# A NaN-skipping row maximum: packed 16-bit keys in a tile of their own, and loads of seven rows

## The chip, the cores and the metric

The kernel runs on one core of a Trainium2 chip. The metric is the device time of one execution, in microseconds (us). The kernel before takes 1284.18 us, the median of three runs (1283.97 to 1284.49).

Of the core's engines three compute here: ScalarE (ACT in the profile), GpSimd (POOL) and VectorE (DVE). SyncE (SP) issues all transfers, loads and stores, in one queue and in program order.

## The reference

The input is a float32 array of 32 x 2048 rows of 2048 numbers, in which about one number in ten is a NaN. The output is the maximum of each row, with NaNs left out:

```python
x = np.random.randn(32, 2048, 2048).astype(np.float32)
x[np.random.rand(32, 2048, 2048) < 0.1] = np.nan

def reference(x, axis):            # axis = -1
    return np.nanmax(x, axis=axis).astype(np.float32)
```

That is 537 MB read for 0.26 MB written. A row that holds nothing but NaNs gives a NaN.

## The kernel before

The 65536 rows are spread over 128 partitions, so that each partition has 512 rows of 8 KB. From here on "a row" means one row in every partition, which is 128 x 8 KB = 1.05 MB of the input.

**How a NaN is made harmless.** [...] the kernel first turns each NaN into the lowest number. It does this on the upper 16 bits of each float (the "key"); the lower 16 bits stay where they are. As a 16-bit integer the key of a NaN (0x7FC0) lies above that of every finite positive number (at most `TOP` = 0x7F7F).

1. ScalarE (L94) reads the key as int16, computes `TOP + 0.25 - key`, multiplies it by a slope `alpha` where it is negative, which is the case for NaNs alone, and writes the result as uint16. `alpha` is chosen so that every NaN gives the one value `TOP + 129`.
2. GpSimd (L102) reads that as uint16, computes `TOP - value` and writes an int16. This gives ordinary keys back unchanged and turns a NaN's key into -129, which is 0xFF7F, the upper half of a very large negative float.
3. VectorE (L110) takes the float32 maximum along each row into `acc`.

Both key steps work in place: they read and write every second 16-bit number of the loaded tile, `[:, 1::2]`, 4 bytes apart. At the end of a group of rows VectorE finds the rows that held only NaNs ("none", L118) and sets bits so that they become NaN ("fin", L127).

**How the work is tiled.** `GROUPS` is a list of groups; a group is a list of tiles, a tile a list of loads, and a load a list of pieces, in rows. A tile is one buffer of `WIDE` = 8 rows (64 KB per partition) of the pool `io`, which has three. Nearly all of the work is tiles of one load of 8 rows, worked on in pieces of 3, 3 and 2 rows: 12 groups of 5 such tiles (40 rows each) and one group of one. The last 24 rows are three groups of one tile each, with loads of 4, 2 or 1 rows and pieces of 2 or 1.

**What sets the order.** Each engine works through its instructions in order and waits for what they need. A piece goes from ScalarE to GpSimd to VectorE. A load into a buffer waits until VectorE has reduced all pieces that the buffer held before, three tiles back. Stores are put off: after each load, if more than one group's result is waiting to be stored, SyncE issues the oldest of these stores (L91) before it issues the next load (L86). A store waits for its group's "fin", and all later loads wait behind it in SyncE's queue. The last stores are at L132.

The functions with their line numbers:

Of the kernel before, what the change touches and what calls it, by code (L numbers as in the profile page):

```python
# [1 line left out]

# [4 lines left out]

FULL = [[3, 3, 2]]
GROUPS = [[FULL] * 5] * 12 + [
    [FULL],
    [[[2, 2], [2], [2]]],
    [[[2], [2], [1], [1], [1], [1]]],
    [[[1], [1], [1], [1], [1], [1], [1], [1]]],
]
WIDE = 8

TOP = 0x7F7F
NAN = 0x7FC0
LOW = -129

EDGE = TOP + 0.25

NONE = -255.0 * 2.0**120


@with_exitstack
def kernel(
    ctx: ExitStack,
    tc: tile.TileContext,
    x: bass.AP,
    axis: bass.AP,
    out: bass.AP,
):

    nc = tc.nc
    P = nc.NUM_PARTITIONS
    f32, i32 = mybir.dt.float32, mybir.dt.int32  # L50
    i16, u16 = mybir.dt.int16, mybir.dt.uint16
    ALU = mybir.AluOpType
    PRELU = mybir.ActivationFunctionType.Prelu

    nd = len(x.shape)
    assert axis in (-1, nd - 1), axis
    D = x.shape[-1]

    xr = x.bitcast(i32).flatten_outer_dims()
    R = xr.shape[0]  # L60
    of = out.bitcast(i32).flatten_outer_dims().rearrange("r c -> (r c)")
    rows = [sum(sum(sum(ld) for ld in tl) for tl in g) for g in GROUPS]
    assert R == P * sum(rows)

    io = ctx.enter_context(tc.tile_pool(name="io", bufs=3))
    res = ctx.enter_context(tc.tile_pool(name="res", bufs=3))
    sing = ctx.enter_context(tc.tile_pool(name="sing", bufs=1))
    top = sing.tile([P, 1], f32)
    nc.vector.memset(top, EDGE)  # L69
    warm = sing.tile([P, 1], f32)  # L70
    nc.scalar.activation(out=warm, in_=top, func=PRELU, alpha=0.5)  # L71

    stores = []
    r0 = 0
    for s, g in zip(rows, GROUPS):
        xg = xr[r0 : r0 + P * s].rearrange("(p s) d -> p (s d)", p=P)
        og = of[r0 : r0 + P * s].rearrange("(p s) -> p s", p=P)
        r0 += P * s
        acc = res.tile([P, s], f32, tag="acc")
        at = 0  # L80
        for tl in g:
            xt = io.tile([P, WIDE * D], i32, tag="xt")
            base = at
            for ld in tl:
                c = sum(ld)
                nc.sync.dma_start(  # L86
                    out=xt[:, (at - base) * D : (at - base + c) * D],
                    in_=xg[:, at * D : (at + c) * D],
                )
                if len(stores) > 1:  # L90
                    nc.sync.dma_start(**stores.pop(0))  # L91
                for c in ld:
                    xp = xt[:, (at - base) * D : (at - base + c) * D]
                    nc.scalar.activation(  # L94
                        out=xp.bitcast(u16)[:, 1::2],
                        in_=xp.bitcast(i16)[:, 1::2],
                        func=PRELU,
                        bias=top,
                        scale=-1.0,
                        alpha=float(TOP - LOW) / (EDGE - NAN),  # L100
                    )
                    nc.gpsimd.tensor_scalar(  # L102
                        out=xp.bitcast(i16)[:, 1::2],
                        in0=xp.bitcast(u16)[:, 1::2],
                        scalar1=-1.0,
                        scalar2=float(TOP),
                        op0=ALU.mult,
                        op1=ALU.add,
                    )
                    nc.vector.tensor_reduce(  # L110
                        out=acc[:, at : at + c],
                        in_=xp.bitcast(f32).rearrange("p (c d) -> p c d", c=c),
                        axis=mybir.AxisListType.X,
                        op=ALU.max,
                    )
                    at += c
        none = res.tile([P, s], i32, tag="none")
        nc.vector.tensor_scalar(  # L118
            out=none,
            in0=acc,  # L120
            scalar1=NONE,
            scalar2=float(0x00C00000),
            op0=ALU.is_equal,
            op1=ALU.mult,
        )
        fin = res.tile([P, s], i32, tag="fin")
        nc.vector.tensor_tensor(  # L127
            out=fin, in0=acc.bitcast(i32), in1=none, op=ALU.bitwise_or
        )
        stores.append(dict(out=og, in_=fin))  # L130
    for st in stores:
        nc.sync.dma_start(**st)  # L132


# [1 line left out]
_INS = ['x', 'axis']  # L136
_OUTS = [((32, 2048), 'float32')]

_NUMBERS = {'axis': -1}


# [26 lines left out]
```

## Time and profile before

| | us |
|---|---|
| median of three runs | 1284.18 |
| the profiled execution, its own time | 1283.97 |
| its span, first to last instruction | 1282.3 |
| busy in the span: ScalarE / GpSimd / VectorE | 1203.3 / 1203.8 / 1142.7 |
| ScalarE waiting for loads, in total (first one) | 67.0 (20.3) |
| VectorE waiting for GpSimd, in total | 135.4 |
| a load of 8 rows, issue to landing, median | 25.8 |

The loads moved 419 GB/s on average over the span. In 40 equal slices of the span the rate is 423 to 448 GB/s in all but the last three, which have 304, 245 and 197 GB/s.

How to read the lines of the profile that follow: "L102 POOL TENSOR_SCALAR xt<-xt ... x122 | 856.0, 7017 | 61.0 <-ACT" is the instruction of line 102 on GpSimd, which wrote the tile xt from xt, 122 times, 856.0 us in all and 7017 ns each; the engine sat idle 61.0 us ahead of these, and mostly until ScalarE had finished something. In the chain and in the timeline the first number is the start in us from the beginning of the span, the second the duration. SPq is SyncE's queue. "DMA share" is the mean busy share of the core's 16 DMA engines.

### The profile page before, as it was taken

How to read it: one execution, taken by the hardware profiler on the slowest of the kernel's cores; microseconds unless marked ns; L12 is line 12 of the kernel's file. 1: busy time of each engine (PE TensorE's matmuls, PEld its weight loads, DVE VectorE, ACT ScalarE, POOL GpSimd, SP SyncE). 2: the span in 40 equal slices, each digit the busy share in tenths (PEclk: the TensorE clock that was granted, in tenths of full speed). 3: DMA queues.
4: the chain of work that ended last, by engine and by line, in shares of the span. 5: the costliest groups of instructions: out<-in, count | busy, mean ns of one | idle time of the engine just before them, and what ended most of it. 6: DMA issues, size and time to landing. Idle time of an engine off the chain costs nothing.

```text
span 1282.3 us, 1065 instructions
## 1 busy us (share of the span) xinstructions
DVE 1142.7 (89%) x234; ACT 1203.3 (94%) x203; POOL 1203.8 (94%) x205
## 2 busy tenths in 40 slices
DVE  0789989989998998998998998998998998998999
ACT  3999999999999999999999999999999999999985
POOL 0999999999999999999999999999999999999996
DMA  9999999999999999999999999999999999999754
GB/s 425 425 425 446 438 425 426 442 440 428 425 438 442 429 425 432 448 429 426 429 448 432 425 429 446 433 423 428 448 430 430 427 448 428 431 427 433 304 245 197
DMA packets 13543, 537.20 MB, mean 419 GB/s; under 512 B 3552, under 2 KB 3552, under 8 KB 3552
## 3 DMA queue, kind: packets, MB, share of 16 engines
q1 hardware_dynamic: 13536, 537.14, 97.1%
q14 instruction: 7, 0.06, 0.0%
HBM read 536.87 MB, written 0.26 MB: 419 GB/s over the span
## 4 chain that ended last, share of the span: by engine, by line
DMA 42%; POOL 23%; DVE 18%; ACT 12%; issue 5%; ACTq 0%; DVEq 0%
DMA xt<-in_x_dram 42%; POOL xt L102 23%; DVE acc L110 18%; ACT xt L94 12%; DVE none L118 1%; DVE fin L127 0%; ACTq L94 0%; DVEq L110 0%; DVEq L127 0%
## 5 line engine op out<-in xcount | busy, mean ns | idle before, releaser
L102 POOL TENSOR_SCALAR xt<-xt 128x6144 int16<-128x6144 uint16 (+2 forms) x201 | 1203.6, 5988 | 69.9 <-ACT xt L94 58.9
L94 ACT ACTIVATE xt<-xt,top 128x6144 uint16<-128x6144 int16 (+2 forms) x201 | 1201.8, 6082 | 67.0 <-DMA xt<-in_x_dram 67.0
L110 DVE TENSOR_REDUCE acc<-xt 128x3 f32<-128x6144 f32 (+2 forms) x201 | 1116.0, 5582 | 135.4 <-POOL xt L102 135.4
L118 DVE TENSOR_SCALAR none<-acc 128x40 int32<-128x40 f32 (+1 forms) x16 | 24.4, 1526 | 0.5
L127 DVE TENSOR_TENSOR fin<-acc,none 128x40 int32<-128x40 int32 (+1 forms) x16 | 4.4, 275 | 0.4
L71 ACT ACT_TABLE_LOAD x1 | 1.3, 1283 | 0.7 <-PEq L149 0.7
L69 DVE MEMSET top<- 128x1 f32 x1 | 0.1, 59 | 0.8 <-PEq L149 0.8
L149 POOL MEMSET const-float32-0.0<- 128x1 f32 x1 | 0.1, 98 | 0.2 <-issue 0.2
L71 ACT ACTIVATE warm<-top 128x1 f32<-128x1 f32 x1 | 0.2, 203 | 0.0
L149 POOL MEMSET const-bfloat16-1.0<- 128x1 bf16 x1 | 0.1, 102 | 0.0
L149 POOL MEMSET const-uint8-127<- 128x1 uint8 x1 | 0.1, 102 | 0.0
L149 POOL MEMSET const-float32-1.0<- 128x1 f32 x1 | 0.1, 98 | 0.0
## 6 DMA issues: line engine op xcount, KB each, us to landing
xt<-in_x_dram SPq DMA_DIRECT2D x12, 1024.0 KB, 9.7
xt<-in_x_dram SPq DMA_DIRECT2D x4, 2048.0 KB, 13.9
xt<-in_x_dram SPq DMA_DIRECT2D x1, 4096.0 KB, 16.1
xt<-in_x_dram SPq DMA_DIRECT2D x61, 25.8
out_dram<-fin SPq DMA_DIRECT2D x12, 20.0 KB, 25.5
out_dram<-fin SPq DMA_DIRECT2D x4, 4.0 KB, 1.4
```

The lines of the kernel that those rows point to most:

```text
L69: nc.vector.memset(top, EDGE)
L71: nc.scalar.activation(out=warm, in_=top, func=PRELU, alpha=0.5)
L94: nc.scalar.activation(out=xp.bitcast(u16)[:, 1::2], in_=xp.bitcast(i16)[:, 1::2], func=PRELU, bias=top, scale=-1.0, alpha=float(TOP - LOW ...
L102: nc.gpsimd.tensor_scalar(out=xp.bitcast(i16)[:, 1::2], in0=xp.bitcast(u16)[:, 1::2], scalar1=-1.0, scalar2=float(TOP), op0=ALU.mult, op1= ...
L110: nc.vector.tensor_reduce(out=acc[:, at : at + c], in_=xp.bitcast(f32).rearrange("p (c d) -> p c d", c=c), axis=mybir.AxisListType.X, op=A ...
L118: nc.vector.tensor_scalar(out=none, in0=acc, scalar1=NONE, scalar2=float(0x00C00000), op0=ALU.is_equal, op1=ALU.mult,)
L127: nc.vector.tensor_tensor(out=fin, in0=acc.bitcast(i32), in1=none, op=ALU.bitwise_or)
L149: nc = _bacc.Bacc("TRN2", target_bir_lowering=False, num_devices=1)
```

## The change

ScalarE no longer writes its 16-bit result over the key in the loaded tile. A new pool `mid` holds two tiles `kt` of `PIECE` = 4 rows of 16-bit numbers (16 KB per partition each). ScalarE reads the keys from xt as before, 4 bytes apart, and writes them side by side into kt. GpSimd reads them side by side from kt and writes the final keys into their places in xt, 4 bytes apart as before. VectorE's part is unchanged. ScalarE may write into a kt tile once GpSimd has read what was there two pieces before.

The tiles of xt go from 8 rows to 7 (56 KB per partition), still three of them. A full tile is one load of 7 rows, in pieces of 4 and 3. There are now 11 groups of 6 full tiles (42 rows each), one of 4 full tiles (28 rows), one of two tiles with smaller loads (14 rows) and one of a tile of 7 rows and a tile of 1 row, in place of 12 groups of 40 rows and four groups of 8.

```diff
-FULL = [[3, 3, 2]]
-GROUPS = [[FULL] * 5] * 12 + [
-    [FULL],
-    [[[2, 2], [2], [2]]],
-    [[[2], [2], [1], [1], [1], [1]]],
-    [[[1], [1], [1], [1], [1], [1], [1], [1]]],
+FULL = [[4, 3]]
+GROUPS = [[FULL] * 6] * 11 + [
+    [FULL] * 4,
+    [[[4], [3]], [[3], [2], [2]]],
+    [[[2], [1, 1], [1], [1], [1]], [[1]]],
 ]
-WIDE = 8
+WIDE = 7
+PIECE = 4
...
     io = ctx.enter_context(tc.tile_pool(name="io", bufs=3))
+    mid = ctx.enter_context(tc.tile_pool(name="mid", bufs=2))
     res = ctx.enter_context(tc.tile_pool(name="res", bufs=3))
...
                     xp = xt[:, (at - base) * D : (at - base + c) * D]
+                    kt = mid.tile([P, PIECE * D], u16, tag="kt")
                     nc.scalar.activation(
-                        out=xp.bitcast(u16)[:, 1::2],
+                        out=kt[:, : c * D],
                         in_=xp.bitcast(i16)[:, 1::2],
...
                     nc.gpsimd.tensor_scalar(
                         out=xp.bitcast(i16)[:, 1::2],
-                        in0=xp.bitcast(u16)[:, 1::2],
+                        in0=kt[:, : c * D],
                         scalar1=-1.0,
```

## The prediction

> **What bounds the kernel now.** I read the page's head first, then the stretches of the run, the groups by shape, the waits of the load queue, the chain, and the timeline of the last 100 us.
>
> Page, head and DMA part (busy time of the three engines; what the queue moved):
> ```profile
> span 1282.3 us, 1065 instructions
> DVE 1142.7 (89%) x234; ACT 1203.3 (94%) x203; POOL 1203.8 (94%) x205
> q1 hardware_dynamic: 13536, 537.14, 97.1%
> ```
> All three engines are near 90% and so tell nothing apart; the DMA engines are at 97.1%. Busy time by stretch (DVE, ACT, POOL, TensorE clock, DMA share, GB/s):
> ```profile
> 100.00:700.00 600.00, 548.46 (x106) 580.96 (x93) 581.30 (x94) 1.00 1.00 433
> 700.00:1180.00 480.00, 438.86 (x85) 464.02 (x75) 464.86 (x75) 1.00 1.00 433
> 1180.00:1283.00 103.00, 97.94 (x34) 81.99 (x23) 89.15 (x24) 1.00 0.62 256
> ```
> Until 1180 us the transfers are the limit: share 1.00, 433 GB/s, so a row of all partitions (128 x 8 KB = 1.049 MB) takes 2.42 us, and an 8-row load 19.36. In the last 103 us the share is 0.62. What each piece costs, groups by shape (busy us, mean ns):
> ```profile
> L94 ACT ACTIVATE xt<-xt,top 128x6144 uint16<-128x6144 int16 x122 | 858.5, 7111 | 58.5 <-DMA xt<-in_x_dram 58.5
> L102 POOL TENSOR_SCALAR xt<-xt 128x6144 int16<-128x6144 uint16 x122 | 856.0, 7017 | 61.0 <-ACT xt L94 56.2
> L110 DVE TENSOR_REDUCE acc<-xt 128x3 f32<-128x6144 f32 x122 | 799.4, 6552 | 135.4 <-POOL xt L102 135.4
> L94 ACT ACTIVATE xt<-xt,top 128x4096 uint16<-128x4096 int16 x67 | 323.3, 4839 | 0.0
> L102 POOL TENSOR_SCALAR xt<-xt 128x4096 int16<-128x4096 uint16 x67 | 318.0, 4746 | 5.3
> L110 DVE TENSOR_REDUCE acc<-xt 128x2 f32<-128x4096 f32 x67 | 295.1, 4409 | 0.0
> ```
> From the differences per row (2048 keys): ACT 2.27 us a row (1.109 ns a key) + 0.29 fixed; POOL 2.27 (1.11) + 0.19; DVE 2.14 + 0.13. A 4-row piece, which is not in this trace, extrapolates to ACT 9.38, POOL 9.29, DVE 8.70.
>
> How near is the buffer loop (load, ACT, POOL, DVE, load into the same buffer)? The chain of waits, one turn:
> ```profile
> 1102.02 25.67 DMA xt<-in_x_dram
> 1127.77 7.16 ACT xt L94
> 1135.01 6.99 POOL xt L102
> 1142.08 7.00 POOL xt L102
> 1149.10 4.89 DVE acc L110
> 1160.01 25.74 DMA xt<-in_x_dram
> ```
> A turn is 57.99 us = 3 loads of 19.33. The load takes 25.7 in it, but the very first load, with nothing ahead of it, took 21.8 (issued 0.74, ACT starts 22.57): 19.36 of transfer + 2.4. So 25.7 holds 3.9 us of queueing: that is the loop's whole slack.
>
> **The Trainium skill.** "ScalarE: Activation LUTs", What ACT_TABLE_LOAD costs: an ACTIVATE with a [128,1] bias takes about 280 ns + 0.833 ns an element. The trace agrees on the fixed part (0.29) and not on the slope (1.109, a third more). "GPSIMD Engine Reference", 3.1: a body of up to two operations is bound by its ports at 1.03 cycles an element, 0.86 ns at 1.2 GHz; the trace has 1.11. Section 7 there: strided reads turn costly above a step of 8 bytes; these keys have a step of 4. "SBUF — State Buffer", Who interferes with whom: a VectorE tensor_scalar or an operation with two SBUF inputs can be blocked for a whole GpSimd instruction. The trace fits: the tiny "none" takes 1.36 us where GpSimd runs and 0.17 at the very end.
>
> Both engines pay the same third more. What they share is a 16-bit read at a 4-byte step and a 16-bit write at a 4-byte step, in place. By the pages the read isn't the costly side (the step is below the GpSimd limit; 4-byte elements run at full ACT speed), so I put the cost on the strided write. That is inference: no packed key operation is in the trace.
>
> **The change part by part.**
> 1. *Loads of 7 rows, pieces 4 and 3.* Transfer 7 x 2.42 = 16.93 us a load, the same per row. Instructions fall from 201 to 152 per engine; that fixed time is hidden behind the transfers.
> 2. *ACT writes packed.* Bounds of a 4-row piece: 9.38 (nothing gained; a loss is excluded, since one strided side of two goes and nothing else changes) to 0.29 + 8192 x 0.833 = 7.11, an estimate from the ScalarE page's slope. I take 7.11: its strided write is gone.
> 3. *POOL reads packed, writes strided.* Bounds for the same reason: 9.29 to 0.19 + 8192 x 0.86 = 7.23, an estimate from the GPSIMD page. I take 9.29: its write stays as it was.
> 4. *New wait.* Two kt tiles: ACT's piece k+2 waits until POOL has read piece k. With pieces 4,3,4,3 one kt tile always carries the 4-row pieces: turn = ACT4 + POOL4 + 0.15 handoffs = 7.11 + 9.29 + 0.15 = 16.55 a load, under 16.93. Behind the waiting ACTIVATE only later ACTIVATEs are queued (loads and stores are on SP), and POOL and DVE wait for those. POOL alone needs 9.29 + 7.02 = 16.31: it fits.
> 5. *The buffer loop.* Pieces are coarser and each is a full stage of latency: load 16.93 + 2.4, ACT4 7.11, POOL4 9.29, then DVE4 8.70 (covering POOL3's 7.02), DVE3 6.55, handoffs 0.2 = 51.2 us. Three transfers are 50.8. The 3.9 us of slack is gone and the loop is 0.4 us over: DMA stops being the limit by a hair, 17.07 a load.
> 6. *The end.* Before, the queue of loads stood behind stores that waited for results (waits of SP: us in total, times, longest):
> ```profile
> SPq L91 <- DVE fin L127: 65.3, 3, 28.4
> ```
> and the timeline shows what that held up:
> ```profile
> 1222.33 4.10 DVE L118 TENSOR_SCALAR none<-acc 128x8 int32<-128x8 f32 x1
> 1231.19 0.34 SPq L91 DMA_DIRECT2D out_dram<-fin  x1
> 1231.58 2.97 SPq L86 DMA_DIRECT2D xt<-in_x_dram  x6
> ```
> Six loads waited for the store at 1231.19. The new groups (28 rows, then 14, then 8) make stores refer to results that are done, or done 3 us later. But the gain is limited: three engines now hang behind the last loads with longer stages, and the DVE, with 2.14 us + fixed cost a row against 2.42 of transfer, hardly catches up. So I count the end from the DVE. Tile 69 (counted from 0, rows up to 490) is the last full one before the ragged tiles; from its first POOL piece on, DVE runs without a gap through 29 rows: 2 pieces of four, 3 of three, 3 of two, 6 of one = 17.40 + 19.65 + 13.23 + 13.62 (2.27 each) = 63.9. Two group ends inside it, at the mean of before's three tail pairs of none + fin, (4.10+0.56+1.88+0.83+1.90+0.42)/3 = 3.2 each, and a last one of 0.35: 6.8.
>
> Sum: first load landed 0.74 + 16.93 + 2.4 = 20.1; tile 69 is 23 turns later, 23 x 51.2 = 1177.6; ACT4 and POOL4 16.5; DVE 63.9 + 6.8; from the last fin to the end of the span as before 2.5 (1279.8 to 1282.3). Together 1287.4 us of span. The profiled execution of before was 1283.97 with a span of 1282.3; with the same 1.7 the time is **1289 us**. That execution lies 0.2 us below the median of 1284.18. The forecast is 0.4% slower: the end saves, the loop gives it back (23 x 0.4 = 9 us).
>
> **Rivals.**
> - *A, packing buys nothing.* If each strided side alone, or the function itself, costs 1.11 ns a key, ACT4 stays 9.38 and the kt turn is 9.38 + 9.29 + 0.15 = 18.82 a load. 20.1 + 69 x 18.82 + 18.8 + 70.7 + 2.5 + 1.7 = 1412 us. For it: the trace has only strided forms. Against: the skill's ACT price, and that both engines have one common slope, which points to a cause in the access. In between, each 0.1 ns of ACT slope above 0.90 (where the kt turn passes 17.07) costs 0.82 x 69 = 57 us.
> - *B, the other side: the loop stays under 50.8.* One mechanism: GpSimd gains too, because working in place was the cost, or its read was. It decides when POOL4 falls below 8.9 us (loop 51.2 - 0.4). At 7.23 the loop is 49.1, transfers bound, tile 69 lands at 0.74 + 2.4 + 70 x 16.93 = 1188.2, and the time is 1188.2 + 14.4 + 70.7 + 4.2 = 1277.5. For it: the identical slope on two different engines. Against: its strided write remains.
> - *C, the read was the cost.* ACT4 9.38, POOL4 7.23: kt turn 16.76, loop 51.2 + 2.27 - 2.06 = 51.4, and 20.1 + 23 x 51.4 + 16.7 + 70.7 + 4.2 = 1294. Against: the 4-byte step is below the page's limit.
>
> **How the numbers follow.** My case 52 in 100, own range 1280 to 1298: a loop 0.4 us shorter gives 1280, and 0.4 longer 1298. Between it and A (ACT gains part) 8, A 17, B 13, C 8, losses that I don't see 2. Measured 0.2% is about what tells a difference from none, 1281.6 to 1286.7. Faster: B 12 and 6 of mine, 0.18; same: 11 of mine, 1 each of B and C, 0.13; slower the rest, 0.69. The range leaves out A and little else: 1276 to 1350.
>
> **What would show it.** ACT 4-row pieces near 7.1 us, POOL near 9.3, DVE 8.7; DMA share 0.99, not 1.00; loads landing about 19.4 us after issue; ACT's waits split between DMA and a little POOL; and no store wait of over 5 us ahead of the last loads. Wrong if ACT stays at 9.4 (ACT waits on POOL each load) or if POOL falls to 7.2 (loads still queue, share 1.00).

## The result, and the profile after

The changed kernel takes 1345.3 us (median of three, 1343.9 to 1346.53), 1.0475 times the time before (95% interval 1.0451 to 1.0499). The profiled execution took 1343.9 us with a span of 1342.1. The direction was forecast, the size was not: the likeliest case said 1289.

The page's head and DMA part of the changed kernel:

```profile
span 1342.1 us, 945 instructions
DVE 1147.9 (86%) x181; ACT 912.5 (68%) x154; POOL 1199.8 (89%) x156
q1 hardware_dynamic: 13680, 537.14, 95.4%
```

ScalarE has become 291 us cheaper (1203.3 before), GpSimd has not (1203.8 before), and the same bytes take longer. By stretch (busy us of DVE, ACT, POOL; TensorE clock; DMA share; GB/s):

```profile
100.00:700.00 600.00, 522.39 (x80) 414.90 (x68) 549.99 (x68) 1.00 0.98 411
700.00:1240.00 540.00, 477.04 (x72) 380.56 (x62) 498.88 (x62) 1.00 0.99 414
1240.00:1343.00 103.00, 91.74 (x23) 55.05 (x15) 81.67 (x16) 1.00 0.59 243
```

The loss lies in the steady part: 411 to 414 GB/s in place of 433. The last 103 us look much as they did before. The share fell by 1 to 2 hundredths and the rate by 4 to 5 in a hundred, so the transfers stand still only for a small part of the loss; mostly they are slower while they run. The groups by shape (busy us, mean ns; idle us before them):

```profile
L104 POOL TENSOR_SCALAR xt<-kt 128x8192 int16<-128x8192 uint16 x71 | 661.9, 9322 | 119.2 <-ACT kt L96 119.1
L112 DVE TENSOR_REDUCE acc<-xt 128x4 f32<-128x8192 f32 x71 | 616.7, 8685 | 190.3 <-POOL xt L104 190.3
L104 POOL TENSOR_SCALAR xt<-kt 128x6144 int16<-128x6144 uint16 x72 | 508.6, 7064 | 5.7
L96 ACT ACTIVATE kt<-xt,top 128x8192 uint16<-128x8192 int16 x71 | 505.7, 7122 | 392.8 <-DMA xt<-in_x_dram 388.7 <-POOL xt L104 4.1
```

ACT 7.12, POOL 9.32, DVE 8.69 us for four rows were forecast as 7.11, 9.29 and 8.70. The wait for kt cost ACT 4.1 us over 71 such pieces. So neither the operations nor the new wait explain the time. ACT waits for loads. One turn of the buffer loop in the chain of waits:

```profile
621.12 22.18 DMA xt<-in_x_dram
...
643.39 7.13 ACT kt L96
...
650.59 9.35 POOL xt L104
...
659.96 15.16 DVE acc L112 x2
...
675.13 21.70 DMA xt<-in_x_dram
```

A turn is 54.0 us here. All its terms but one are the forecast's. The load takes about 22 us where the forecast had 16.93 + 2.4 = 19.3; its median over the run is 21.7:

```profile
xt<-in_x_dram SPq DMA_DIRECT2D x70, 7168.0 KB, 21.7
```

The question for the experiments is why.

### The profile page after: what moved, and what is told of

Read it like the earlier page. It is cut to its first block, busy times and chain, and to the rows that moved or that the text cites. A ratio compares the mean times of both kernels' runs of the same rounds, so it can differ in the third digit from the quotient of the medians.

```text
span 1342.1 us, 945 instructions
## 1 busy us (share of the span) xinstructions
DVE 1147.9 (86%) x181; ACT 912.5 (68%) x154; POOL 1199.8 (89%) x156
## 4 chain that ended last, share of the span: by engine, by line
DMA 38%; DVE 27%; POOL 17%; ACT 13%; issue 4%; another core or an unknown queue 0%; ACTq 0%; SPq 0%; DVEq 0%; POOLq 0%
DMA xt<-in_x_dram 38%; DVE acc L112 26%; POOL xt L104 17%; ACT kt L96 13%; DVE none L120 1%; DVE fin L129 0%; ACTq L96 0%; SPq L87 0%; DVEq L112 0%; POOLq L104 0%
## 5 line engine op out<-in xcount | busy, mean ns | idle before, releaser
L104 POOL TENSOR_SCALAR xt<-kt 128x8192 int16<-128x8192 uint16 (+3 forms) x152 | 1199.6, 7892 | 131.0 <-ACT kt L96 124.5
L112 DVE TENSOR_REDUCE acc<-xt 128x4 f32<-128x8192 f32 (+3 forms) x152 | 1108.2, 7333 | 190.3 <-POOL xt L104 190.3
L96 ACT ACTIVATE kt<-xt,top 128x8192 uint16<-128x8192 int16 (+3 forms) x152 | 911.0, 6037 | 414.7 <-DMA xt<-in_x_dram 397.9
L120 DVE TENSOR_SCALAR none<-acc 128x42 int32<-128x42 f32 (+3 forms) x14 | 35.1, 2508 | 0.4
L129 DVE TENSOR_TENSOR fin<-acc,none 128x42 int32<-128x42 int32 (+3 forms) x14 | 6.2, 440 | 0.4
## 6 DMA issues: line engine op xcount, KB each, us to landing
xt<-in_x_dram SPq DMA_DIRECT2D x70, 7168.0 KB, 21.7
```

The lines of the kernel that those rows point to most:

```text
L96: nc.scalar.activation(out=kt[:, : c * D], in_=xp.bitcast(i16)[:, 1::2], func=PRELU, bias=top, scale=-1.0, alpha=float(TOP - LOW) / (EDGE ...
L104: nc.gpsimd.tensor_scalar(out=xp.bitcast(i16)[:, 1::2], in0=kt[:, : c * D], scalar1=-1.0, scalar2=float(TOP), op0=ALU.mult, op1=ALU.add,)
L112: nc.vector.tensor_reduce(out=acc[:, at : at + c], in_=xp.bitcast(f32).rearrange("p (c d) -> p c d", c=c), axis=mybir.AxisListType.X, op=A ...
L120: nc.vector.tensor_scalar(out=none, in0=acc, scalar1=NONE, scalar2=float(0x00C00000), op0=ALU.is_equal, op1=ALU.mult,)
L129: nc.vector.tensor_tensor(out=fin, in0=acc.bitcast(i32), in1=none, op=ALU.bitwise_or)
```

## The experiments

In what follows the *lead* of a load is the time from its issue to the landing of the load ahead of it: the time it has in the queue behind another. From the issue and landing times in the trace its median was 6.4 us before and 3.9 us after. A load that only waits its turn lands 16.93 us, its own transfer, after the one ahead of it. The theory is that the loop, now longer than three transfers, leaves loads too little lead, and that a load with little lead runs slowly on top. The main rivals are that ScalarE's and GpSimd's new traffic slows the transfers, and that GpSimd or the kt wait sets the pace.

**Two transfers a tile.** This gives the loads more lead, lets ScalarE start when four rows have landed in place of seven, and leaves every engine instruction alone.

```diff
-FULL = [[4, 3]]
+FULL = [[4], [3]]
```

> The changed kernel with each full tile loaded in two transfers of 4 and 3 rows; all engine instructions as they were. Theory (the buffer loop is longer than three transfers, and a load that isn't queued well ahead is slow as well): the 4-row part lands after 9.68 + 2.4 us, so the loop is about 44 us against 50.8, the transfers are the limit again, DMA share 1.00 and 433 GB/s, 16.9 us a tile; 1272 us in all. Rival (the packets are slowed by what ScalarE and GpSimd do with the new tile, queued or not): still 16.9 x 1.03 us a tile and DMA at about 415 GB/s, some 1310 us. Rival (GpSimd or the wait for kt sets the pace): no change, 1345 us.

Measured: 1276.98 us, 0.9943 times the kernel before (0.9927 to 0.996). By stretch:

```profile
100.00:1100.00 1000.00, 908.98 (x138) 737.76 (x118) 961.43 (x118) 1.00 1.00 431
```

The share is 1.00 and the rate 431 GB/s, with the same packed tile and GpSimd as busy as ever. The same groups of instructions have the same durations (7122, 9325 and 8685 ns). So the new traffic does not slow the transfers, and GpSimd at 16.4 us a tile doesn't set the pace. In that stretch every load had at least 9 us of lead. The time is 5 us above the expected 1272 and the rate 2 GB/s under the expected 433; the packets, below, say why.

**Shorter pieces.**

```diff
-FULL = [[4, 3]]
+FULL = [[3, 2, 2]]
```

> The changed kernel with pieces of 3, 2 and 2 rows in place of 4 and 3; loads as they were. Theory (loop too long): load 19.4 + ACT 5.40 + POOL 7.06 + DVE 6.54 + 4.40 + 4.40 = 47.2 us, 3.6 under the 50.8 of three transfers, so loads are queued ahead again, about 23 us from issue to landing with DMA share 1.00; 1278 us. Rival (packets slowed by the engines' new traffic): 415 GB/s, some 1310 us. Rival (GpSimd sets the pace: 16.6 us a tile with the third fixed cost): no gain over 1345 us.

Measured: 1311.01 us, 1.0209 times before (1.0193 to 1.0224). The number is the one of the rival with slowed packets, but the waits say otherwise (total us, times, longest):

```profile
ACT kt L96 <- POOL xt L104: 345.5, 150, 4.1
ACT kt L96 <- DMA xt<-in_x_dram: 18.3, 1, 18.3
```

ACT never waited for a load but the first. It waited for kt, and the chain shows a turn without any load in it:

```profile
612.85 5.42 ACT kt L96
...
618.35 7.04 POOL xt L104
...
625.47 4.77 POOL xt L104
...
630.26 5.42 ACT kt L96
```

With three pieces on two kt tiles, ACT's 3-row piece waits for POOL's first 2-row piece of the tile before, which comes behind POOL's 3-row piece: 5.42 + 7.04 + 4.77 and 0.2 of handoffs = 17.4 us a load. None of the three expectations had this. The run had taken away one limit and run into another, so its time says nothing on the theory. Its loads do say something. They were issued 17.4 us apart, as that turn allowed, and no engine waited for them, yet from issue to landing they took as long as in the changed kernel:

```profile
xt<-in_x_dram SPq DMA_DIRECT2D x70, 7168.0 KB, 21.6
```

Their median lead was 4.2 us. So a load is slow here without being the limit of the kernel.

**Without the packed tile.**

```diff
-                        out=kt[:, : c * D],
+                        out=xp.bitcast(u16)[:, 1::2],
...
-                        in0=kt[:, : c * D],
+                        in0=xp.bitcast(u16)[:, 1::2],
```

> The new geometry (7-row loads, pieces of 4 and 3) without kt: both key steps in place as in the kernel before. Theory: ACT back at 9.38 us for 4 rows, which adds 2.26 us to the loop; with loads still at 21.7 us the loop is 55.8 us, 18.6 a load, and the time about 1400 us; GpSimd stays at 9.3. Rival (the slow loads come from the traffic of the packed tile, which is gone): loads take 19.4, loop 53.5, about 1345 us. If the loop weren't the cause of the loss, the time would be near 1285 us.

Measured: 1379.29 us in one run, between the two. The groups show ACT at its old rate, and the DMA issues show loads that are still slow at 20.9 us, though less so:

```profile
L94 ACT ACTIVATE xt<-xt,top 128x8192 uint16<-128x8192 int16 x71 | 666.4, 9386 | 151.9 <-DMA xt<-in_x_dram 148.7 <-DVE none L118 2.5 <-DVE acc L110 0.8
```

```profile
xt<-in_x_dram SPq DMA_DIRECT2D x70, 7168.0 KB, 20.9
```

9.39 + 9.27 + 15.23 + 20.9 + 0.2 of handoffs = 55.0 us, 18.3 a load. The median lead was 2.7 us. The geometry alone would cost 95 us, more than the 61 of the change as a whole; the packed write gives part of it back.

**Loads and VectorE alone.** Both key steps are left out, and the maximum is taken over the bits as integers; there are two tile buffers, as in the diff, and in a further run one.

```diff
-    io = ctx.enter_context(tc.tile_pool(name="io", bufs=3))
+    io = ctx.enter_context(tc.tile_pool(name="io", bufs=2))
...
-                    nc.scalar.activation(
...
-                    nc.gpsimd.tensor_scalar(
...
-                        in_=xp.bitcast(f32).rearrange("p (c d) -> p c d", c=c),
+                        in_=xp.rearrange("p (c d) -> p c d", c=c),
```

> Loads and VectorE alone: both key steps left out (the maximum is taken over the bits as int32), two tile buffers in place of three, so that the loop is load + 15.2 us of reducing, near two transfers of 16.93, as the loop of the changed kernel is near three. If loads are slow whenever they are issued just before the one ahead of them ends: about 21.7 us from issue to landing, 18.5 us a load, about 1355 us in all. If it takes ScalarE's and GpSimd's traffic to slow them: 19.4 us, 17.35 a load, about 1275 us.

> As the run with loads and VectorE alone (both key steps left out), with one tile buffer: every load of 7 rows is issued with nothing ahead of it in the queue. If starting on an empty queue is itself slow: 21.7 us from issue to landing, 37 us a load. If the extra time comes only from being issued in the last microseconds of the load ahead: 19.4 us (16.93 + 2.4, as the first load of the kernel before suggests) to 20.1 (as the first load of the changed kernel), 35 us a load.

Measured: 1359.3 us with two buffers and 2535.57 us with one. The DMA issues, first with two and then with one buffer (KB each, median us to landing):

```profile
xt<-in_x_dram SPq DMA_DIRECT2D x70, 7168.0 KB, 21.8
```

```profile
xt<-in_x_dram SPq DMA_DIRECT2D x70, 7168.0 KB, 19.7
```

With ScalarE and GpSimd silent the loads are as slow as in the changed kernel (21.8), at a median lead of 3.1 us; alone in the queue they take 19.7. So it takes no traffic of ScalarE or GpSimd to make a load slow. A load behind another one took 2 us longer from issue to landing than a load on an empty queue; part of that is time behind the other, so the intervals between landings, below, say more.

**Is it the lead, or only the turn in the queue?** With the 3-row piece first, the stages behind the landing are 1.1 us shorter.

```diff
-FULL = [[4, 3]]
+FULL = [[3, 4]]
```

> The changed kernel with the pieces of each full tile in the order 3, 4 in place of 4, 3; loads and everything else as they were. From the landing to the last reduce this is ACT 5.42 + POOL 7.06 + POOL 9.32 + DVE 8.69 + handoffs 0.1 = 30.6 us, 1.1 less than with 4 first. If a load waits only for its turn in a queue (19.7 us when alone), the loop is 30.6 + 19.7 = 50.3, under the 50.8 of three transfers: DMA share 1.00, 16.93 a load, about 1278 us. If a load issued less than about 5 us before the landing of the one ahead costs some 21.6 us whatever the loop would allow: 52.2 us a turn, 17.4 a load, DMA share 0.99, about 1308 us.

Measured: 1344.73 us (1340.14 to 1348.56), 1.0479 times before (1.0461 to 1.0496): no gain, and neither number. The timeline shows what came in between:

```profile
566.19 8.22 DVE L120 TENSOR_SCALAR none<-acc 128x42 int32<-128x42 f32 x1
```

At a group's end the tiny "none" sat 8.2 us on VectorE. GpSimd's two pieces ran from 557.94 to 574.37, the second from 565.08, and "none" ended with it. Five of the eleven group ends went this way (8.2 to 8.5 us). That fits the Trainium skill, "SBUF — State Buffer", Who interferes with whom, on VectorE operations that are blocked for a GpSimd instruction. To take that out, all 70 full tiles were put into one group, in both orders of pieces:

```diff
-GROUPS = [[FULL] * 6] * 11 + [
-    [FULL] * 4,
+GROUPS = [
+    [FULL] * 70,
...
-    res = ctx.enter_context(tc.tile_pool(name="res", bufs=3))
+    res = ctx.enter_context(tc.tile_pool(name="res", bufs=1))
```

> Pieces in the order 3, 4 as in the run before this one, but with all 70 full tiles in one group, so that no group's end (none and fin on VectorE) falls into the steady part. What is to be compared is the stretch from 100 to 1100 us. If a load waits only for its turn in the queue: loop 30.6 + 19.7 = 50.3, under three transfers, DMA share 1.00 at 433 GB/s. If a load issued less than about 5 us ahead costs 21.6 us: 52.2 a turn, 17.4 us a load, about 422 GB/s.

> The control of the run with one group: pieces 4, 3 as in the changed kernel, all 70 full tiles in one group. If the group ends cost the changed kernel nothing in its steady part: about 411 GB/s from 100 to 1100 us, 17.9 us a load, as with its groups. If they were what made its loads late: 431 GB/s or more.

Measured: 1318.2 us with 3 first, 1343.58 us with 4 first, one run each. By stretch, 3 first and then 4 first:

```profile
100.00:1100.00 1000.00, 869.55 (x116) 710.63 (x115) 938.90 (x116) 1.00 0.99 420
```

```profile
100.00:1100.00 1000.00, 848.28 (x113) 697.61 (x113) 918.80 (x113) 1.00 0.98 412
```

The control answers first: 412 GB/s, as the changed kernel has over the same stretch (413), so its own group ends cost it nothing in the steady part. With 3 first the rate is 420 GB/s, 17.47 us from one landing to the next, and loads take 21.6. A load that only waits its turn would have given 433. It is the small lead that makes loads slow: this loop had room for 50.3 and took 52.4.

The loads one by one say the same. I took those of 7 rows issued between 100 and 1100 us, from the changed kernel, the six runs so far that load 7 rows in one transfer behind another load, and the run with GpSimd's packed write further down. By how much was the interval between two landings longer than 16.93 us of transfer?

| lead of the load, us | loads | longer by, mean us |
|---|---|---|
| under 2 | 23 | 2.9 |
| 2 to 3 | 68 | 1.7 |
| 3 to 4 | 136 | 1.0 |
| 4 to 5 | 132 | 0.3 |
| 5 to 6 | 30 | 0.2 |
| over 6 | 64 | 0.04 |

The trace's packets agree. A packet carries one partition's part of a load, and each of the 16 DMA engines carries eight packets of a full load. Before, packets of 65,536 bytes took 2.420 us in the median and 2.422 in the mean. After, packets of 57,344 bytes took 2.116 in the median, the same rate, but 2.183 in the mean. Around 600 to 645 us, where I followed them, nearly all of the slow ones (2.3 to 3.9 us) were among the first two that an engine carried of a new load. In the run with one buffer, where each load starts on an empty queue, the first packet of each engine took 2.79 us in the mean and the other seven 2.12. So a slow first packet belongs to a load's start, and a lead of 4 us doesn't yet hide it, while 6.4 does. Why it takes that much was not tried. With two transfers a tile the packets had their usual length, 1.218 us for 4 rows and 0.914 for 3, but eight of each make 17.06 us in place of 16.93, which is about that run's 431 GB/s in place of 433.

**What makes the keys slow.** The prediction had put the third that both engines paid on the strided write. Two runs test this: ScalarE writes with stride into a tile of its own, and the sides are changed over so that GpSimd's write is packed. In the second, VectorE reduces what ScalarE wrote, and GpSimd's keys are left out of the result.

```diff
-FULL = [[4, 3]]
+FULL = [[2, 2], [2, 1]]
...
-    [[[4], [3]], [[3], [2], [2]]],
+    [[[2, 2], [2, 1]], [[2, 1], [2], [2]]],
...
-PIECE = 4
+PIECE = 2
...
-                    kt = mid.tile([P, PIECE * D], u16, tag="kt")
+                    kt = mid.tile([P, PIECE * D], i32, tag="kt")
...
-                        out=kt[:, : c * D],
+                        out=kt[:, : c * D].bitcast(u16)[:, 1::2],
...
-                        in0=kt[:, : c * D],
+                        in0=kt[:, : c * D].bitcast(u16)[:, 1::2],
```

> ScalarE writes its keys into a tile of their own, but every second 16-bit number of it, and GpSimd reads them so (loads of 4 and 3 rows, pieces of 2 and 1). If the strided write is what made ScalarE slow (my reading): 4.84 us for 2 rows, as in the kernel before. If working in place made it slow: 3.70 us. GpSimd 4.75 either way.

```diff
                     nc.scalar.activation(
-                        out=kt[:, : c * D],
+                        out=xp.bitcast(u16)[:, 1::2],
...
                     nc.gpsimd.tensor_scalar(
-                        out=xp.bitcast(i16)[:, 1::2],
-                        in0=kt[:, : c * D],
+                        out=kt[:, : c * D].bitcast(i16),
+                        in0=xp.bitcast(u16)[:, 1::2],
```

> The two sides changed over: ScalarE writes in place with stride, GpSimd reads with stride and writes its keys packed into kt; VectorE then reduces what ScalarE wrote, so the second key step is left out of the result. If GpSimd's slope comes from its strided write: 7.2 us for 4 rows in place of 9.3. If it is GpSimd's own rate for this operation, 9.3. ScalarE 9.38 for 4 rows. The time says nothing here.

Measured (1442.91 and 1275.56 us), the group in question of each run:

```profile
L96 ACT ACTIVATE kt<-xt,top 128x4096 uint16<-128x4096 int16 x217 | 1040.9, 4846 | 188.2 <-POOL xt L104 177.3 <-DMA xt<-in_x_dram 10.9
```

```profile
L104 POOL TENSOR_SCALAR kt<-xt 128x8192 int16<-128x8192 uint16 x71 | 498.4, 7020 | 347.6 <-ACT xt L96 339.1 <-issue 8.5
```

ScalarE pays the full 4.85 us with its strided write in another tile (3.70 for the same pieces written packed, in the version below), so working in place is not the cause. GpSimd drops from 9.32 to 7.02 us with a packed write and a strided read. Both pay for the strided write: 1.11 ns a key in place of 0.83. GpSimd's strided read costs nothing (9.27 us with it, without the packed tile; 9.32 with a packed read). ScalarE reads with stride in every run, so what its read costs is not shown. The first of these runs is slow for another reason: two kt tiles with ACT 4.85 and POOL 4.75 us in turn limit it to about 19.3 us a tile.

The second run settles one more rival, that a transfer of 7 rows is slow as such; two transfers a tile had changed the size as well as the lead. Here the loads are those of the changed kernel, but VectorE doesn't wait for GpSimd, the loop is shorter and the median lead 9.2 us:

```profile
100.00:1100.00 1000.00, 896.09 (x139) 964.83 (x119) 726.29 (x119) 1.00 1.00 433
```

**A version with a shorter end.**

```diff
-FULL = [[4, 3]]
+FULL = [[2, 2], [2, 1]]
...
-    [[[4], [3]], [[3], [2], [2]]],
+    [[[2, 2], [2, 1]], [[2, 1], [2], [2]]],
...
-PIECE = 4
+PIECE = 2
...
-    mid = ctx.enter_context(tc.tile_pool(name="mid", bufs=2))
+    mid = ctx.enter_context(tc.tile_pool(name="mid", bufs=4))
```

> Full tiles loaded in transfers of 4 and 3 rows, worked on in pieces of 2, 2, 2 and 1, with four kt tiles of 2 rows. GpSimd needs 3 x 4.77 + 2.47 + handoffs = 16.9 us a tile against 17.0 of transfers at 431 GB/s, so the transfers stay the limit, and the last rows leave the engines some 7 us earlier than with pieces of 4 (landing of a 4-row load to its last reduce 17.7 in place of 25 us): 1265 us. If GpSimd falls behind, it sets the pace with the same 16.9 to 17.3 us a tile and the end grows: 1277 to 1290.

Measured: 1274.04 us, 0.9918 times before (0.9902 to 0.9935), the fastest of all that compute the whole result. It gained 3 us on the run with two transfers a tile, not 12. GpSimd waited for nothing after its first input:

```profile
POOL xt L104 <- ACT kt L96: 16.4, 1, 16.4
```

Its four instructions a tile, 3 x 4.76 + 2.48, with 0.08 us between them make 17.07 us, just over the 17.03 of the transfers at 431 GB/s, so it had a backlog at the end. That is the mechanism of the second of the two expectations (1277 to 1290), though the time lies 3 us below its range.

## Why the prediction was right and wrong

**What bounds the kernel** held: transfers. The 3.9 us of slack were counted with the time of a load that is alone, and not all of it could be used: one group with 3 first was 0.5 us under three transfers by that count (50.3 against 50.8) and still ran at 420 GB/s. **Steps 1 to 4** held with their numbers: ACT 7.12, POOL 9.32, DVE 8.69 us, a kt turn that fits within a load, and the cause behind them (the strided write), which was only argued then and is shown now.

**Step 5 is where the forecast failed in size.** Its mechanism was right: coarser pieces make the loop longer than three transfers. Mis-sized was the term "load 16.93 + 2.4", taken from the first load of the run, which starts on an empty queue. That term is within 0.4 us for a load that is alone (19.7 measured) and for one with much lead it doesn't matter, but in between a load takes 21.7: it lands 17.8 us after the one ahead of it, in place of 17.07. The sign that went with the term, loads landing about 19.4 us after issue, failed too. The turn was 53.4 us on average (three intervals of 17.8) and not 51.2. It cost 2.2 us on each of 23 turns, and the first load landed 0.7 us late: tile 69's first POOL piece ended at 1265.0 us where the forecast had 1214.2, which is 50.8 us late. The forecast had loop and transfers as two limits of which the longer one counts; the run with one group and 3 first shows that the rate falls while the loop is still the shorter one.

**Step 6** was good to 4 us. From there to the end of the span 77.1 us passed, against 63.9 + 6.8 + 2.5 = 73.2. The difference is "none" and "fin" at the ends of groups:

```profile
1290.24 5.63 DVE L120 TENSOR_SCALAR none<-acc 128x28 int32<-128x28 f32 x1
1302.19 3.31 DVE L129 TENSOR_TENSOR fin<-acc,none 128x28 int32<-128x28 int32 x1
```

With the later pair (1.03 and 0.44) that makes 10.4 us where 6.5 were counted. The claim that stores would hold up no load for more than 3 us was wrong: the last five loads waited for the store at 1305.53, which SyncE had waited 25.0 us to issue.

```profile
SPq L92 <- DVE fin L129: 25.0, 1, 25.0
```

It cost nothing, because VectorE worked without a gap from 1281.63 us to the last "none", and the last of these loads had landed at 1323.51. 50.8 and 3.9 added to the forecast span of 1287.4 give the 1342.1 that was measured.

**The rivals.** None of A, B and C came about. The case between mine and A, in which ScalarE gains only in part, would have given the measured time too, and the range up to 1350 was wide enough for it. That the measured time lies inside that range is luck: ScalarE gained all that was forecast, and the loss came from loads. The likeliest case's own range, 1280 to 1298, allowed for 0.4 us of error in the loop where 2.2 came, so it was drawn too narrow.

## What to carry to other kernels

When a buffer loop comes near the limit of its transfers, don't price a load at what it takes alone: measured with 3 to 4 us of lead, it took 2 us longer from issue to landing, and landed 1 us later after the one ahead of it than its transfer takes. A lead of over 6 us was enough here. Count each stage's latency before making pieces coarser, and if the buffers can't grow, split the transfers: this kept the changed kernel's instructions and turned 4.8% slower into 0.6% faster. And where two engines hand 16-bit data on through a few small tiles, write out their turn for the very sequence of piece sizes, since 4, 3 and 3, 2, 2 on two tiles differ.

## What was not expected of the hardware

- A 7-row load took 19.7 us alone and 21.6 to 21.8 with 3 to 4 us of lead. With 6.4 us (8-row loads) and with 9.2 (7-row loads) the transfers ran without loss at 433 GB/s.
- A 16-bit write at a step of 4 bytes cost ScalarE and GpSimd the same third, 1.11 ns in place of 0.83 a key, and a read at that step cost GpSimd nothing.
- A VectorE operation on 42 numbers a partition took 8.2 us at one group's end, until the GpSimd instruction beside it was done, and 0.19 us in the run where GpSimd had no work.
